# A sparse branch's q, k and v made in the gate part and passed through DRAM, and a merged sum kept in DRAM

## The chip, the cores and the metric

The kernel runs on one core of one Trainium2 chip. The metric is device time in microseconds (us), the median of several runs. The engines are TensorE (PE, with its weight loads PEld), VectorE (DVE), ScalarE (ACT), GpSimd (POOL) and SyncE (SP), which here issues nearly all DMAs, in order. TensorE's granted clock is shown as a share of 2.4 GHz: 1.00 is the upper level, 0.50 the lower one (1.2 GHz).

## The reference

One decoder layer for 1024 tokens of width 1024, with three token mixers over one input projection: A, sparse attention (8 heads of 64; an indexer scores all keys, and each query keeps its 256 best), B, latent attention (8 heads), and M, cross-attention to 256 memory tokens. Each result is multiplied by silu of a gate path and projected to 1024 columns; three sigmoid gates weigh the three, and one output projection goes back to the residual stream.

```python
h = rms_norm(x, g_norm[layer])
proj = h @ w_in[layer]
(q_a, k_a, v_a, q_i, k_i, w_i, z_a, c_q, c_kv, k_rope, z_b, q_m, z_m,
 gate_logits) = jnp.split(proj, split_at, axis=-1)
q_a = partial_rope(rms_norm(q_a.reshape(b, s, A_HEADS, A_HEAD_DIM), g_qn_a[layer]), ...)
k_a = partial_rope(rms_norm(k_a.reshape(b, s, A_HEADS, A_HEAD_DIM), g_kn_a[layer]), ...)
o_a = dsa_attention(q_a, k_a, v_a, q_i, k_i, w_i)      # top 256 keys of each query
...
ys = jnp.stack([o_a * silu(z_a), o_b * silu(z_b), o_m * silu(z_m)], axis=0)
branch = jnp.einsum('nbsw,nwd->nbsd', ys, w_branch[layer])
gates = jax.nn.sigmoid(gate_logits.reshape(b, s, N_BRANCH, D_MODEL))
merged = jnp.einsum('bsnd,nbsd->bsd', gates, branch)
x = x + merged @ w_out[layer]
```

## The kernel before

Every float32 operand is split into a high and a low part (`wsplit`, L246 to L251: ScalarE rounds, VectorE or GpSimd subtracts, as the list `ws` says), and a product is three matmuls (`mm3`, L276 to L279). The transposed normalised input h stays in SBUF all along (tiles hTh, hTl).

The stages follow one another: memory branch; latent branch; the indexer's scores (tiles idx); the gate and branch part; sparse attention; merge and output projection. A framework places the instructions on the engines' queues: program order gives the priority, and an instruction whose operands are expected earlier can be put ahead. Each engine, and SP, then works in the order so fixed.

The **top-k** (`topk_group`) finds the 256th largest score of each row bit by bit: 32 counting passes over six token blocks. Blocks 3, 4 and 6 are counted on ScalarE (tile names ka...), blocks 2, 5 and 7 on VectorE (kd...), L1039. For the upper 16 bits VectorE's passes read bf16 copies (kdh). After the passes each block needs some ten operations of VectorE, and its mask is stored to DRAM (s_msk). `run_topk` hands these steps out: after each group of products it adds the group's planned time on TensorE times TKC (0.44) to an account, and issues steps while the account is positive, each at a planned price. What is left at the end of the part is issued there.

The **gate and branch part**: `branch` for M, then for B. For four blocks of 128 columns it makes z (48 matmuls each), multiplies it with the branch's result (osb, from DRAM) and splits it (tiles yh, yl). Then for eight blocks of output columns and two halves of the tokens it makes a branch product (12 matmuls of 512 columns in a PSUM bank) and multiplies it with the gate (tile tg, from DRAM, two buffers). `emit_b` writes the first branch's result to a sum in SBUF (acc), `emit_m` has GpSimd add the second and stores the sum to DRAM (s_acc). Between them z of branch A is made for three of four blocks (`z_early`, NZG 3) and stored.

The **sparse attention** works by head pairs, 32 units in all (four pairs, two heads, four pairs of token blocks). `qkv_gen` makes q, k and v of a pair (8 token blocks of 24 matmuls with 384 columns), with norms, rotation and split: for the first pair ahead of the loop, for the others in pieces between the units. The filler (`Filler`) puts gate products of branch A between the units, 8 jobs of 16 steps of three matmuls, as many at a place as PFA says. Masks are loaded at the head of the stage (L1385).

In the **merge**, `branch` runs for A: z of the fourth block, the four y tiles, the branch products, the stored sum (tile ac) added, and then the output projection.

## Time and profile before

| | us |
|---|---|
| median of three runs | 1429.53 (1427.94 to 1429.56) |
| span of the profiled execution | 1427.6 |
| TensorE busy | 1366.2 (96%) |
| VectorE busy | 967.5 (68%) |
| ScalarE busy | 687.7 (48%) |
| GpSimd busy | 270.2 (19%) |

The page of the profile gives busy times over the whole span. The questions here are about stages, so the stretches matter: for each, how long TensorE was busy, and at which granted clock. TensorE is never far from busy; what can be won or lost is its idle time and the time at the lower clock.

### The profile page before, as it was taken

The numbers are of one execution on the slowest core, as the hardware profiler recorded it, in microseconds if no ns is written. First come the engines' busy times: TensorE is split into PE (matmuls) and PEld (weight loads), VectorE is DVE, ScalarE is ACT, GpSimd is POOL, SyncE is SP. The second block draws the span as 40 slices with busy tenths as digits, with TensorE's granted clock in tenths as the row PEclk, the third lists the DMA queues.
The fourth block names the chain that finished last, engine by engine and source line by source line (L and its number), as shares of the span: only waits on it lengthen the run. The fifth ranks groups of instructions, "written<-read, shape, count | busy, mean of one in ns | idle before, by whom it ended". The sixth has DMA issues, their size and how long they took to land.

```text
span 1427.6 us, 20798 instructions
## 1 busy us (share of the span) xinstructions
PE 1366.2 (96%) x7440; PEld 1173.0 (82%) x7440; DVE 967.5 (68%) x2409; ACT 687.7 (48%) x1488; POOL 270.2 (19%) x254
## 2 busy tenths in 40 slices
PE   7999999999999999898988998899999999999998
PEld 5998888888888889786867886689899898877887
DVE  5935446678888861479879678777777868836511
ACT  6635433356666651464576563224555535633200
POOL 3150003511102000200232335331202011003200
PEclk9999999999999999999998999999999999999999
DMA  7411222311111120210224325630201001185622
GB/s 245 136 45 52 78 59 86 114 56 41 49 56 53 45 93 20 67 45 23 89 79 151 97 75 182 193 85 9 67 23 45 31 15 45 38 276 184 210 96 74
DMA packets 124631, 122.34 MB, mean 86 GB/s; under 512 B 20336, under 2 KB 90224, under 8 KB 124528
## 3 DMA queue, kind: packets, MB, share of 16 engines
q1 hardware_dynamic: 123952, 118.92, 26.8%
q10 hardware_dynamic: 576, 2.10, 0.4%
q8 instruction: 58, 0.95, 0.3%
q14 instruction: 45, 0.37, 0.1%
HBM read 87.93 MB, written 33.06 MB: 85 GB/s over the span
## 4 chain that ended last, share of the span: by engine, by line
PE 68%; DVE 15%; ACT 6%; issue 4%; DMA 4%; POOL 1%; SPq 1%; ACTq 0%; DVEq 0%; POOLq 0%
PE f L277 5%; PE f L278 5%; PE f L279 4%; DVE kdj L1039 3%; PE a L277 3%; PE a L278 3%; PE a L279 3%; PE o L277 2%; PE o L278 2%; PE o L279 2%; ACT kag L1049 2%; PE br L277 2%; PE br L278 2%; PE br L279 2%; DVE sz L1292 1%
## 5 line engine op out<-in xcount | busy, mean ns | idle before, releaser
L1049 ACT ACTIVATE kag<-idx,kaT 128x512 bf16<-128x512 f32 (+2 forms) x96 | 82.9, 864 | 56.0 <-DVE kaT L1077 39.4
L277 PE MATMUL f<-hTh,f_0h 128*128 128x512 f32 x184 | 77.0, 419 | 1.9 <-ACT f_0h L248 1.2
L277 PE MATMUL f<-hTh,f_1h 128*128 128x512 f32 x184 | 75.6, 411 | 1.3 <-ACT f_1h L248 1.3
L279 PE MATMUL f<-hTh,f_0l 128*128 128x512 f32 x184 | 74.4, 405 | 0.6 <-POOL f_0l L251 0.6
L278 PE MATMUL f<-hTl,f_0h 128*128 128x512 f32 x184 | 74.5, 405 | 0.0
L279 PE MATMUL f<-hTh,f_1l 128*128 128x512 f32 x184 | 74.0, 402 | 0.0
L278 PE MATMUL f<-hTl,f_1h 128*128 128x512 f32 x184 | 73.6, 400 | 0.0
L1568 DVE TENSOR_TENSOR xr<-o,xr 128x512 f32<-128x512 f32 x16 | 11.1, 691 | 64.0 <-PE o L279 64.0
L1223 ACT ACTIVATE irl<-is 128x512 f32<-128x512 f32 (+1 forms) x80 | 37.6, 524 | 24.2 <-DVE idx L1229 15.5
L1526 POOL TENSOR_TENSOR ac<-ac,tg 128x512 f32<-128x512 f32 x16 | 23.5, 1469 | 128.6 <-DMA wo_3r<-in_w_out_dram 109.9
L1039 DVE TENSOR_SCALAR_CACHE_REDUCE kdj<-kdh,kdT 128x384 bf16<-128x384 bf16 (+2 forms) x48 | 46.3, 965 | 0.8
L1039 DVE TENSOR_SCALAR_CACHE_REDUCE kdj<-idx,kdT 128x384 bf16<-128x384 f32 (+2 forms) x48 | 46.2, 963 | 0.6
L369 ACT ACTIVATE fo<-f 128x512 f32<-128x512 f32 x48 | 28.7, 599 | 35.2 <-PE f L279 29.0
L279 PEld LDWEIGHTS f<-hTh,f_0l 128*128 128x128 f32 x184 | 35.2, 191 | 7.9 <-POOL f_0l L251 1.1
L1229 DVE SCALAR_TENSOR_TENSOR idx<-irl,wi,idx 128x1024 f32<-128x1024 f32 (+5 forms) x42 | 40.6, 966 | 1.5 <-ACT irl L1223 0.4
L277 PEld LDWEIGHTS f<-hTh,f_0h 128*128 128x128 f32 x184 | 35.1, 191 | 7.2 <-ACT f_0h L248 1.4
L279 PEld LDWEIGHTS f<-hTh,f_1l 128*128 128x128 f32 x184 | 34.8, 189 | 7.0 <-DVE f_1l L251 0.6
L277 PEld LDWEIGHTS f<-hTh,f_1h 128*128 128x128 f32 x184 | 35.0, 190 | 6.7 <-ACT f_1h L248 2.1
L278 PEld LDWEIGHTS f<-hTl,f_1h 128*128 128x128 f32 x184 | 34.9, 190 | 5.2
L278 PEld LDWEIGHTS f<-hTl,f_0h 128*128 128x128 f32 x184 | 35.3, 192 | 4.3
L1412 ACT ACTIVATE asq<-a 128x256 f32<-128x256 f32 x32 | 12.3, 384 | 51.1 <-PE a L279 50.9
L1266 DVE SCALAR_TENSOR_TENSOR sz<-sz,z 128x512 f32<-128x512 f32 x24 | 16.4, 683 | 27.7 <-ACT sz L1265 27.7
(1215 smaller groups left out, 4862.1 us busy)
## 6 DMA issues: line engine op xcount, KB each, us to landing
s_tg<-fo SPq DMA_DIRECT2D x48, 256.0 KB, 2.0
tg<-s_tg SPq DMA_DIRECT2D x48, 256.0 KB, 3.0
f_0r<-in_w_in_dram SPq DMA_DIRECT2D x23, 256.0 KB, 3.0
f_1r<-in_w_in_dram SPq DMA_DIRECT2D x23, 256.0 KB, 2.9
xx<-in_x_dram SPq DMA_DIRECT2D x8, 512.0 KB, 7.3
osb<-s_o SPq DMA_DIRECT2D x8, 512.0 KB, 3.8
s_acc<-acc SPq DMA_DIRECT2D x16, 256.0 KB, 2.4
ac<-s_acc SPq DMA_DIRECT2D x16, 256.0 KB, 3.4
```

The source lines that it names most:

```text
L277: nc.tensor.matmul(ps, ah, bh, start=start, stop=False)
L278: nc.tensor.matmul(ps, ah, bl, start=False, stop=False)
L279: nc.tensor.matmul(ps, al, bh, start=False, stop=stop)
L369: nc.scalar.activation(o, ps, AF.Tanh, scale=0.5)
L1039: nc.vector.tensor_scalar(out=junk, in0=src[t], scalar1=T[:, i:i + 1], scalar2=0.0, op0=op, op1=ALU.add, accum_out=cnt[:, i:i + 1])
L1049: nc.scalar.activation(junk, idx[t], AF.Sign, bias=T[:, i:i + 1], accum_out=cnt[:, i:i + 1])
L1223: nc.scalar.activation(rl[:, k0:k0 + m], sp[:, 0:m], AF.Relu)
L1229: i_ = nc.vector.scalar_tensor_tensor(out=acc[:, 0:n], in0=rl[:, 0:n], scalar=wc, in1=acc[:, 0:n], op0=ALU.mult, op1=ALU.add)
L1266: zi[0] = nc.vector.scalar_tensor_tensor(out=sz, in0=sz, scalar=1.0, in1=pz[j], op0=ALU.add, op1=ALU.mult)
L1292: i_ = (nc.gpsimd if n and PMUL else nc.vector).tensor_tensor(sz, osb[:, cs], sz, op=ALU.mult)
L1412: nc.scalar.activation(sq.rearrange("p h d -> p (h d)"), ps[:, 0:256], AF.Square)
L1526: nc.gpsimd.tensor_tensor(ac, ac, tg, op=ALU.add)
```

## The change

Four things. The q, k and v of branch A are made by a new function `qkv` inside the gate and branch part, one pair each after the y tiles of the first branch, after those of the second, and twice between the last blocks of z; they are normalised, rotated and split there, stored to DRAM, and loaded in the attention by `load_gen`, the next pair ahead of time (k twice, side by side). The sum of the branches is no longer in SBUF: `emit_b` stores it, `emit_m` loads it, VectorE adds, and it is stored again. The top-k's passes on VectorE all read float32, and a step's planned price and the rate (TKC 0.33) are other. All four blocks of z of branch A are made in the gate part. Beside that: three buffers for tg, osb by halves, own weight buffers for z and branch weights (six), and another spread of the filler (PFA, and FWA weight buffers 6 for 4).

```diff
-TKC = 0.44
+TKC = 0.33
-PFA = (0, 1, 1, 0, 0, 1)
-FWA = 4
+PFA = (1, 1, 1, 0, 0, 1)
+FWA = 6
...
-                yield n / (960 if src is idx else 1900) + 0.1
+                    yield n / 960 + 0.2
...
-            osb = wk.tile([P, S], F32, tag="osb", name=f"osb{n}_{w}", bufs=ob)
-            nc.sync.dma_start(osb, o_T[w * P:(w + 1) * P, :])
+                osb = wk.tile([P, 512], F32, tag="osb", name=f"osb{n}_{w}_{j}", bufs=ob)
+                nc.sync.dma_start(osb, o_T[w * P:(w + 1) * P, cs])
...
         def emit_b(d, j, tg, pb):
-            i_ = nc.vector.scalar_tensor_tensor(out=acc[d][j], in0=tg, scalar=1.0, in1=pb, op0=ALU.add, op1=ALU.mult)
-            run_topk(i_, 2.6 if (2, d) in gates_done else 7.7)
+            i_ = nc.vector.scalar_tensor_tensor(out=tg, in0=tg, scalar=1.0, in1=pb, op0=ALU.add, op1=ALU.mult)
+            nc.sync.dma_start(acc_at(d, j), tg)
+            run_topk(i_, 2.6)
 
         def emit_m(d, j, tg, pb):
-            i_ = nc.vector.scalar_tensor_tensor(out=tg, in0=tg, scalar=1.0, in1=pb, op0=ALU.add, op1=ALU.mult)
-            run_topk(i_, 2.6 if (1, d) in gates_done else 7.7)
-            nc.gpsimd.tensor_tensor(acc[d][j], acc[d][j], tg, op=ALU.add)
-            nc.sync.dma_start(s_acc[d * P:(d + 1) * P, j * 512:(j + 1) * 512], acc[d][j])
+            ac = wk.tile([P, 512], F32, tag="ac", name=f"am{d}_{j}")
+            nc.sync.dma_start(ac, acc_at(d, j))
+            nc.vector.scalar_tensor_tensor(out=tg, in0=tg, scalar=1.0, in1=pb, op0=ALU.add, op1=ALU.mult)
+            i_ = nc.vector.tensor_tensor(tg, tg, ac, op=ALU.add)
+            nc.sync.dma_start(acc_at(d, j), tg)
+            run_topk(i_, 2.6)
+
+        def qkv(p):
+            c = P * p
+            cols = [(C_QA + c, P), (C_KA + c, P), (C_VA + c, P)]
+            ws[:] = WSQ
+            pieces = [wload(wpool, f"a{p}w{kp}", [(wview(w_in, 2 * kp, 2, c0, n), n) for c0, n in cols], 2, 384)
+                      for kp in range(4)]
+            ws[:] = WSG
+            for j in range(2):
+                ...
+                for i in range(4):
+                    tb = 4 * j + i
+                    ps = ps_turn(f"a{p}_{tb}", GAB)[:, 0:384]
+                    for kt in range(NK):
+                        ah, al = h_lhs(kt, tb)
+                        wh, wl = pieces[kt // 2]
+                        mm3(ps, ah, al, wh[:, kt % 2, :], wl[:, kt % 2, :], kt == 0, kt == NK - 1)
+                    ...
+                    nc.scalar.copy(vst[:, i, 0::3, :], pv)
+                    i_ = nc.vector.tensor_tensor(vst[:, i, 1:3, :], pv, f(vst[:, i, 0::3, :]), op=ALU.subtract)
+                    run_topk(i_, 4.2)
+                rsqrt_mean(rr, ss, 1.0 / 64)
+                ...
+                nc.vector.tensor_tensor(qs[:, :, :, 1, :], xq, f(qs[:, :, :, 0, :]), op=ALU.subtract)
+                nc.sync.dma_start(s_va[p][j], f(vst).rearrange("p t e d -> p (t e d)"))
+                nc.sync.dma_start(s_ka[p][j], xk.rearrange("p t h d -> p (t h d)"))
+                nc.sync.dma_start(s_qa[p][j], f(qs).rearrange("p t h e d -> p (t h e d)"))
...
-        branch(2, C_ZM, wpool, wk, yp, s_om, emit_b, run_topk, ob=OBG, mid=lambda: early(0, ZE[0]))
-        branch(1, C_ZB, wpool, wk, yp, s_o[1], emit_m, run_topk, ob=OBG, mid=lambda: early(ZE[0], ZE[1]))
...
+        branch(2, C_ZM, wpool, wk, yp, s_om, emit_b, run_topk, tgb=3, ob=2, mid=lambda: qkv(0))
+        branch(1, C_ZB, wpool, wk, yp, s_o[1], emit_m, run_topk, tgb=3, ob=2, mid=lambda: qkv(1))
+        early(0, 2)
+        qkv(2)
+        early(2, 4)
+        qkv(3)
...
-        def qkv_gen(p):
...
+        def load_gen(p):
             yield 1
+            qs = hd.tile([P, NT, 2, 2, 64], FR, tag="qs", name=f"aqs{p}")
+            kd = hd.tile([P, NT, 2, 2, 64], F32, tag="kd", name=f"akd{p}")
...
+            for j in range(2):
+                for e in range(2):
+                    nc.sync.dma_start(kd.rearrange("p t h e d -> p (t h) e d")[:, 8 * j:8 * j + 8, e],
+                                      s_ka[p][j].rearrange("p (g d) -> p g d", g=8))
+            for src, dst in ((s_qa, f(qs).rearrange("p t h e d -> p (t h e d)")),
+                             (s_va, f(vst).rearrange("p t e d -> p (t e d)"))):
+                for j in range(2):
+                    nc.sync.dma_start(dst[:, 1024 * j:1024 * j + 1024], src[p][j])
```

## Rows read from the trace of the kernel before

**Rows 1.** Stretches: start:end, length, busy us of each engine, PEclk, DMA share, GB/s.
```profile
290.00:505.00 215.00, 214.09 (x1358) 187.16 (x1356) 180.74 (x535) 138.70 (x335) 21.57 (x24) 1.00 0.17 49
...
590.00:672.30 82.30, 74.87 (x347) 58.47 (x347) 71.67 (x118) 45.59 (x93) 8.84 (x11) 0.96 0.16 45
672.30:732.70 60.40, 57.70 (x250) 46.27 (x250) 53.18 (x131) 39.79 (x86) 18.32 (x16) 1.00 0.25 77
732.70:786.60 53.90, 46.56 (x193) 37.98 (x192) 45.57 (x109) 35.00 (x73) 14.14 (x11) 0.91 0.41 134
786.60:842.60 56.00, 56.00 (x241) 45.05 (x241) 39.17 (x86) 32.05 (x67) 20.55 (x16) 1.00 0.27 81
842.60:902.60 60.00, 48.45 (x193) 37.75 (x192) 48.86 (x102) 28.38 (x54) 30.52 (x23) 0.94 0.54 172
902.60:915.40 12.80, 12.77 (x48) 10.29 (x49) 10.54 (x19) 2.21 (x4) 6.48 (x8) 0.87 0.66 203
915.40:953.00 37.60, 35.91 (x194) 35.08 (x193) 27.67 (x70) 10.43 (x23) 7.66 (x8) 0.95 0.31 87
953.00:968.00 15.00, 12.05 (x62) 10.29 (x60) 11.29 (x34) 6.28 (x14) 6.82 (x6) 0.89 0.42 103
968.00:1249.60 281.60, 278.25 (x1714) 252.63 (x1713) 221.99 (x692) 149.90 (x355) 33.66 (x28) 1.00 0.12 35
1249.60:1289.80 40.20, 38.91 (x167) 30.53 (x166) 17.23 (x24) 14.92 (x23) 0.00 (x0) 1.00 0.83 268
1289.80:1334.50 44.70, 44.14 (x193) 35.94 (x192) 28.19 (x40) 15.23 (x24) 20.61 (x15) 1.00 0.58 191
```

**Rows 2.** TensorE's waits, 672.3 to 915.4 us: total, times, longest.
```profile
PE br L277 <- DVE tg L1345: 8.3, 4, 4.3
...
PE br L277 <- DVE acc L1341: 7.3, 1, 7.3
```

**Rows 3.** VectorE's groups, 672.3 to 915.4: count, busy us, mean ns, idle before.
```profile
L1039 DVE TENSOR_SCALAR_CACHE_REDUCE kdj<-idx,kdT 128x1024 bf16<-128x1024 f32 x16 | 20.4, 1274 | 0.2
...
L1039 DVE TENSOR_SCALAR_CACHE_REDUCE kdj<-kdh,kdT 128x1024 bf16<-128x1024 bf16 x11 | 14.0, 1277 | 0.3
```

**Rows 4.** DMA issues over the span: count, KB each, median us to landing.
```profile
tg<-s_tg SPq DMA_DIRECT2D x48, 256.0 KB, 3.0
...
s_acc<-acc SPq DMA_DIRECT2D x16, 256.0 KB, 2.4
...
xqp<-s_qb SPq DMA_DIRECT2D x8, 384.0 KB, 3.3
```

**Rows 5.** VectorE's groups in the sparse attention, 915.4 to 1249.6 us.
```profile
L1413 DVE TENSOR_REDUCE ass<-asq 128x4 f32<-128x256 f32 x32 | 13.3, 417 | 17.9 <-ACT asq L1412 17.7
...
L1444 DVE TENSOR_TENSOR akd<-axk,arr 128x512 f32<-128x512 f32 x16 | 10.8, 683 | 0.2
...
L1419 DVE TENSOR_TENSOR avst<-a,avst 128x128 fp32r<-128x128 f32 x32 | 9.1, 285 | 3.9 <-ACT avst L1418 3.8
...
L426 DVE TENSOR_TENSOR ar_0rp<-axk,cos_a 128x64 f32<-128x64 f32 x8 | 1.8, 224 | 0.0
...
L251 DVE TENSOR_TENSOR a1w0l<-a1w0r,a1w0h 128x768 fp32r<-128x768 f32 x1 | 1.0, 959 | 0.5 <-ACT a1w0h L248 0.5
```

**Rows 6.** Timeline of SP's queue at the end of the top-k.
```profile
937.78 0.32 SPq L1385 DMA_DIRECT2D msk<-s_msk  x1
...
938.15 0.43 SPq L393 DMA_DIRECT2D f_0r<-in_w_in_dram  x1
```

**Rows 7.** Timeline of VectorE, block 6's last part: first and last of nine.
```profile
929.29 1.09 DVE L1085 TENSOR_SCALAR_CACHE_REDUCE kai<-kas 128x896 bf16<-128x896 bf16 x1 [1.08 <-DMA s_msk<-kae]
...
935.60 0.22 DVE L1126 TENSOR_TENSOR kae<-kae,cmask 128x128 bf16<-128x128 bf16 x1
```

**Rows 8.** Timelines on the way into the merge: first load, third y tile's split.
```profile
1249.78 0.32 SPq L1288 DMA_DIRECT2D osb<-s_o  x1
...
1268.31 1.29 DVE L1297 TENSOR_TENSOR yl<-sz,yh 128x512 fp32r<-128x512 f32 x2
```

More of the change, by code (lines that the diff above doesn't have):

```diff
@@ L41 @@
 PFQ = 4
-NZG = 3
 YD = True
@@ L229, in hybrid_kernel @@
     s_acc = dr.tile([D, S], F32, name="s_acc")
+    s_qa, s_ka, s_va = ([[dr.tile([P, n], F32, name=f"s_{c}a{p}_{j}") for j in range(2)] for p in range(4)]
+                        for c, n in (("q", 1024), ("k", 512), ("v", 1024)))
     def rsqrt_mean(dst, ss, inv_n):
@@ L264, in wload @@
             o += w
-        hi = tile(FR, "wp", pool_raw[1], nm + "h")
-        lo = tile(FR, "wp", pool_raw[1], nm + "l")
+        tag, bufs, width = kind or ("wp", pool_raw[1], width)
+        hi = tile(FR, tag, bufs, nm + "h", width)
+        lo = tile(FR, tag, bufs, nm + "l", width)
         wsplit(hi, lo, raw)
@@ L1033, in topk_group, with test @@
         ri = tk.tile([P, nb], I32, name=nm + "r")
[L1035 to L1045 removed]
+        def test():
+            if not act:
+                for i, t in enumerate(ts):
+                    n = (t + 1) * P
+                    junk = tk.tile([P, S], BF, tag="tke", name=f"{nm}j{t}", bufs=1)[:, 0:n]
+                    nc.vector.tensor_scalar(out=junk, in0=idx[t], scalar1=T[:, i:i + 1], scalar2=0.0, op0=ALU.is_ge,
+                                            op1=ALU.add, accum_out=cnt[:, i:i + 1])
+                    yield n / 960 + 0.2
                 return
@@ L1065, in topk_group @@
         nc.vector.memset(T, 0.0)
-        yield from test(high)
+        yield from test()
         if act:
@@ L1072, in topk_group @@
         for b in range(30, -1, -1):
-            yield from test(high if b > 15 else idx)
+            yield from test()
             if act:
@@ L1241, in hybrid_kernel @@
     z_done = set()
+    wkind = [None]
     def z_part(n, w, zc, wpool, wk, zb=2, loaded=None):
@@ L1334, in hybrid_kernel, with acc_at @@
         pool_raw[:] = [2, 8, 768]
-        ap_ = ph.enter_context(tc.tile_pool(name="acc", bufs=1, reuse_waits="tile"))
+        wkind[0] = ("wz", 6, 512)
         yp = ph.enter_context(tc.tile_pool(name="y", bufs=1, reuse_waits="tile"))
         wk = ph.enter_context(tc.tile_pool(name="gwork", bufs=2, reuse_waits="tile"))
-        acc = [[ap_.tile([P, 512], F32, name=f"acc{d}_{j}") for j in range(2)] for d in range(NK)]
+        def acc_at(d, j):
+            return s_acc[d * P:(d + 1) * P, j * 512:(j + 1) * 512]
```

157 lines of the change are left out of this document (49 added, 108 removed).

## The prediction

> **What bounds the kernel now.** I read the busy times first: TensorE has work in 96% of the span, by the table of the page above. The change moves matrix products and adds none, so it can only win time in which TensorE stands still or runs at its lower clock. So I cut the span into stages and looked, in each, at the stage's length, TensorE's busy time and the granted clock [rows 1]. A pace is needed to turn counts into time: the undisturbed z stretch did 240 products of 512 columns in 56.0 us at clock 1.00, that is 0.233 us each; by columns a product of 384 (q, k, v) then needs 0.175 us.
>
> Lost time by stage, [rows 1]: the indexer stretch from 590 us has 82.3 - 74.9 = 7.4 us idle and a clock of 0.96, 3.3 us more: 10.7. The gate and branch part (672.3 to 915.4) needs 528 z and 384 branch products at 0.233 us, 212.8 us, and some 2 us of indexer products; it lasts 243.1, so 28.3 are lost, nearly all in its two branch stretches. The first q, k, v (915.4 to 953) takes 37.6 for 192 x 0.175 = 33.6: 4.0. The start of the attention loop (to 968): 4.6 (3.0 idle, the rest clock). The loop to 1249.6: 3.4 in 282 us. From there to the merge (1289.8): 40.2 for 164 products, 38.3: 1.9. The merge's 192 products take 44.7, nothing lost. Sum: 52.9 us. That is the most that the stretch from 590 us on can give back.
>
> The waits of TensorE say why the branch stretches lose: it waits for VectorE's product of gate and branch (tg, acc) [rows 2]. The granted clock falls to 0.91 and 0.94 in those stretches [rows 1], so each long wait is paid for a second time at the lower clock. Behind the waits are two things. VectorE is busy for 45.6 of 53.9 us there [rows 1], mostly with the top-k's counting passes [rows 3]; and a tg tile has two buffers: the next load (3.0 us, [rows 4]) is issued only after the sum has read the old tile.
>
> **The change, part by part.**
>
> *Counting passes.* The bf16 copies go; all 32 passes of VectorE's group read f32. The row: 128x1024 takes 1277 ns in bf16 and 1274 in f32 [rows 3]. So this costs nothing. The planner however had priced a bf16 pass at half, so in the kernel before it packed twice the work into a planned microsecond; the true prices and the lower rate (0.33 for 0.44) take that pressure away. For a planned 2.6 us of a branch product, the top-k then gets 0.86 us of VectorE at about true price, where before it got 1.14 us of plan, twice that in true time while bf16 lasted. The indexer stretch, where VectorE is busy 71.7 of 82.3 us [rows 1], gets about half the passes: I take 8 us lost for 10.7 (6 to 11).
>
> By the Trainium skill (VectorE: DVE Perf Modes, section The perf-mode tier table) a tensor_scalar in bf16 runs at four elements a cycle and in f32 at two. It would make 16 f32 passes of the three tiles cost some 23 us of VectorE more than the bf16 ones, an estimate from that ratio and the rows; the counting form in this trace shows no difference at all, so the sum leaves it out.
>
> *q, k, v into the gate part.* 768 products, 134.4 us of TensorE, leave the attention stage, and the last 48 products of z (11.2 us) leave the way into the merge. Both go into the gate part: 212.8 + 145.6 = 358 us of products there. Their cost is zero only if VectorE follows. Per token block of 4.2 us TensorE it has four operations, 0.42 and three of 0.28 to 0.29, 1.27 us [rows 5], 1.1 for its share of rotation, scaling and splitting (a quarter of twelve operations of about 0.25 and two of 0.68), 0.5 for its share of the weight splits (four of 0.96 for eight blocks [rows 5]) and 1.4 planned us of top-k: 4.3, just full. The branch stretches have room (0.68 + 0.86, in the second 1.36 + 0.86, of 2.8 us), the z stretches more. The sum over the part: the 197 us busy of now, plus about 100 of moved work at the same overlap, is under 300 of 358.
>
> *The sum in DRAM, three tg buffers.* Now 16 stores and 16 loads more, and the add moves from POOL to VectorE (0.68 us a piece). A tg tile lives for its load, 3.0 us, the products, 1.4, and a store of 2.4 [rows 4], with waits about 7.5: over three buffers 2.5 us, just under the 2.8 us of one branch product. Each store waits on SP for VectorE's add, and behind it in SP's order stand the next loads of tg, sum and branch weights, for which TensorE waits. The bytes stay under the work: 10 MB written for q, k, v and 8 MB moved for the sum, in a part whose branch stretches already ran at 134 and 172 GB/s [rows 1]; q, k, v add 24 stores and 32 loads on SP, at some 0.4 us of issue [rows 6] 22 us of a queue that is idle most of 600 us. I take 12 us lost in the gate part for 28.3. Bounds: 5, as in its z stretches (3 to 4 lost in 129 us), and 25, if the round trip of the sum paces the second branch.
>
> *The boundary to the attention.* Before, the first q, k, v hid the end of the top-k: its last tile ran until 935.8, the mask was stored, the load of it issued at 937.8, and the filler's weights behind that on SP [rows 6], all under products. Now nothing of that kind follows the last q, k, v. The plan's accounts: 340 planned us (before: 195; q, k, v 134 and the fourth z 10 more) x 0.33 = 112 units; the steps' planned prices are 92 for VectorE's passes and 35 for the rest, less 10 done in the indexer, 117. So 5 are left over. The last tile needed nine operations, 6.1 us of VectorE between 929.3 and 935.8 [rows 7], for 3.5 units: 1.7 us a unit. The last q, k, v carries 11 units, 19 us, beside its own 23 us, in 33.6 us: VectorE comes out 8 us late, 8.5 more for the rest, then the mask's store and load, 2.4 + 3.0 by tiles of that size [rows 4]: 22 us after the last product. K too must come from DRAM (bounded by the nearest load, 3.3 us for 384 KB in pieces of 384 bytes [rows 4]) and can't before the weights' memory is free. Against that stand one filler job (48 products, 11 us) and 3 us of transposes and scores. That leaves 8 us, and the clock falls: with the first chain of softmax I take 14 us lost, for 8.6 now (4.0 + 4.6). Bounds 3 and 28: no backlog, or filler weights that queue behind the masks on SP, as in [rows 6].
>
> By the Trainium skill (DMA: Bandwidth & Descriptors, Specifications) pieces under 512 bytes fall below line rate; K is read in pieces of 256. If that doubled the load it would cost some 3 us, once, an estimate; the row with pieces of 384 bytes shows 3.3 us, no such doubling, and the other pairs are loaded far ahead.
>
> *The attention loop* loses the q, k, v work of TensorE, VectorE and ACT alike. What is left per unit is the filler, spread wider (115 of 128 steps inside it, 82 before), and its own products. The nearest stage is the latent branch's loop, built the same way, 0.9 us idle in 215 at 181 us of VectorE [rows 1]; the sparse loop has 222.0 us of VectorE now [rows 1], loses some 70 (24 token blocks at 1.27 + 1.1, the two heads' K scaling, the filler's splits, which fall to POOL) and keeps about 150 in about 200 us (281.6, less 100 of q, k, v, plus 18 of filler). I take 4 us for 3.4 (0 to 12).
>
> *Into the merge.* Here cover is given away: 116 filler products and the 48 of z, 38 us [rows 1], stand there now while the last heads are stored, loaded, multiplied and split; 13 filler steps, 9 us, remain. The loads begin where the attention ends, at 1249.8, and the first three of four y tiles are ready 20 us on [rows 8]; now in halves with two buffers, about 21 us to the last. 9 us of filler and up to 10 us of partial sums in five banks cover most: I take 7 lost for 1.9 (1 to 16).
>
> Sum: 8 + 12 + 14 + 4 + 7 = 45 for 52.9, 8 us less. The profiled span is 1427.6 and the median of the runs 1429.5, 1.9 above. 1427.6 - 8 + 1.9 = 1421.5 us.
>
> **The rivals.**
> Cover everywhere: top-k in time at the boundary (6), gate part 7, merge 3, indexer 8, loop 3: 27 lost, 26 gained, 1403.5. For it: VectorE has 60 us of room over the gate part. Against it: the end of the top-k is where the room isn't.
> Slower, the boundary: the top-k's backlog holds the masks, SP holds the filler's weights behind them, and TensorE stands for the whole 22 us and pays the clock: 30 lost there, 1437.5. It decides against the change from about 25 us on. For it: the order on SP in [rows 6]. Against it: the filler could be loaded first.
> The round trip: the second branch stays paced by its loads, as now: gate part 25 lost, 1434.5. For it: 2.5 us against 2.8 is thin and SP issues in order.
> The change doesn't do what it says, because the order of issue leaves the stretches as they are: 1429.5.
> The Trainium skill's f32 rule (VectorE: DVE Perf Modes), with 23 us more of VectorE on the path, would give up to 1444; with 1277 against 1274 ns it gets no chance.
>
> **How the numbers follow.** Forecast 0.45 (1413 to 1430 by its own bounds), cover 0.20, boundary 0.20, round trip 0.12, nothing 0.03. The range 1403 to 1440 reaches from the cover rival to a little beyond the boundary one. A measurement tells about 0.2%, 2.9 us, from no change. Faster: three quarters of the forecast, all of the cover case and a little of the others, 0.59; within: 0.15; slower: 0.26.
>
> **What would show it.** Right: TensorE's waits for tg and acc down from 15.6 us to a few, clock near 1.00 in the branch stretches; a TensorE gap of about 10 us with a fall of the clock after the last q, k, v, ended by masks or K; some 7 us idle ahead of the merge's first branch product. Wrong: branch stretches that still wait for tg or for the sum's loads; a boundary over 25 us (then it is slower); or no gap at either place (then 1403). If the loop itself idles by more than 12 us, my comparison with the latent branch's loop is at fault.

## The result and the profile after

The changed kernel takes 1475.98 us (1474.21 to 1480.0, four runs) where the kernel before takes 1428.74 beside it: 1.034 times as long, with a 95% interval of 1.0321 to 1.036. The forecast was 1421.5, the range ended at 1440. The profiled execution has a span of 1473.8 us, 46.2 more than before.

First the page of the profile after: busy times over the span, and the DMA line.

```profile
PE 1374.4 (93%) x7440; PEld 1173.9 (80%) x7440; DVE 952.7 (65%) x2381; ACT 682.2 (46%) x1465; POOL 261.3 (18%) x248
...
DMA packets 153960, 154.86 MB, mean 105 GB/s; under 512 B 38400, under 2 KB 108288, under 8 KB 153856
```

TensorE has the same 7440 matmuls as before, and the other engines less work; TensorE is busy 8 us longer and its share fell from 96 to 93%, so the loss is idle time and low clock again. The DMAs move 154.86 MB where they moved 122.34. The stretches of the changed kernel, with the columns of [rows 1]: the indexer; the whole gate and branch part; in it the first branch, the z of the second, the second branch, the first z of branch A and the fourth q, k, v; the boundary, up to the first transposed probabilities; the attention loop; the way into the merge; the merge's products.

```profile
590.00:672.00 82.00, 74.22 (x356) 59.61 (x356) 69.33 (x107) 47.62 (x100) 4.47 (x9) 0.97 0.16 48
...
672.00:1058.80 386.80, 367.06 (x1727) 317.76 (x1726) 263.40 (x699) 171.43 (x363) 106.08 (x88) 0.98 0.44 138
...
752.00:800.00 48.00, 44.92 (x194) 35.86 (x193) 29.66 (x89) 22.56 (x50) 12.19 (x10) 1.00 0.61 194
800.00:851.60 51.60, 45.95 (x193) 35.67 (x193) 35.38 (x67) 24.51 (x48) 17.20 (x13) 1.00 0.51 146
...
887.00:937.70 50.70, 46.77 (x193) 36.45 (x191) 35.84 (x96) 19.67 (x42) 15.94 (x15) 0.97 0.69 225
937.70:967.00 29.30, 25.25 (x97) 20.43 (x98) 18.79 (x43) 14.97 (x28) 3.65 (x4) 0.88 0.64 194
...
1024.80:1058.80 34.00, 33.99 (x193) 33.63 (x191) 24.51 (x76) 9.15 (x20) 4.36 (x4) 1.00 0.21 76
1058.80:1102.80 44.00, 14.83 (x48) 11.04 (x49) 28.52 (x67) 9.26 (x18) 7.81 (x8) 0.57 0.68 193
1102.80:1302.40 199.60, 198.22 (x1227) 167.79 (x1226) 157.91 (x459) 123.35 (x273) 18.02 (x14) 1.00 0.29 84
1302.40:1325.20 22.80, 9.27 (x41) 7.21 (x39) 11.87 (x18) 7.83 (x13) 0.00 (x0) 0.81 0.86 280
1325.20:1381.00 55.80, 50.42 (x193) 37.86 (x194) 31.13 (x41) 16.14 (x25) 24.41 (x15) 0.93 0.66 212
```

Read by the prediction's own rule (idle time, and busy time at the lower clock; for the gate part and the merge length less products at 0.233 us, 0.175 for q, k, v):

| stretch | lost before | forecast | lost after |
|---|---|---|---|
| indexer | 10.7 | 8 | 7.8 idle, 2.2 by the clock: 10.0 |
| gate and branch part | 28.3 | 12 | 386.8 - 358.4 = 28.4 |
| boundary to the attention | 8.6 | 14 | 29.2 idle, 6 by the clock: 35 |
| attention loop | 3.4 | 4 | 1.4 |
| into the merge, and its products | 1.9 | 7 | 78.6 - 231 x 0.233 = 24.8 |
| sum | 52.9 | 45 | 99.6 |

The sum grew by 46.7, the span by 46.2. Two places hold it, the boundary (+26) and the merge (+23), and the gate part gave nothing back. TensorE's waits (total, times, longest) name what stands there; the first row is the boundary's, the second the merge's, the others the gate part's.

```profile
PE akt L1442 <- DMA akd<-s_ka: 21.5, 2, 16.3
...
PE br L273 <- ACT b0w0h L241: 13.6, 1, 13.6
...
PE z L273 <- ACT kag L1042: 4.2, 1, 4.2
PE z L275 <- POOL z1w_4l L244: 4.1, 3, 2.0
PE br L273 <- DVE tg L1327: 3.8, 5, 2.6
...
PE br L273 <- DVE tg L1320: 0.9, 1, 0.9
```

The 8.3 and 7.3 us of [rows 2] are down to 3.8 and 0.9. At the boundary the queue of SP shows why TensorE stood 16.3 us for K of the first pair, which had lain in DRAM for 300 us (timeline: start, length, DMA):

```profile
1059.02 1.31 SPq L1426 DMA_DIRECT2D akd<-s_ka  x2
1066.35 0.33 SPq L1113 DMA_DIRECT2D s_msk<-kde  x1
...
1071.46 0.32 SPq L1378 DMA_DIRECT2D s_ka<-a_1xk  x1
...
1073.49 0.32 SPq L1379 DMA_DIRECT2D s_qa<-a_1qs  x1
1073.85 0.53 SPq L1426 DMA_DIRECT2D akd<-s_ka  x1
1077.41 0.33 SPq L1113 DMA_DIRECT2D s_msk<-kae  x1
1077.78 0.53 SPq L1426 DMA_DIRECT2D akd<-s_ka  x1
...
1086.09 0.32 SPq L1113 DMA_DIRECT2D s_msk<-kae  x1
...
1088.14 0.32 SPq L1412 DMA_DIRECT2D msk<-s_msk  x1
1088.50 0.81 SPq L389 DMA_DIRECT2D f_0r<-in_w_in_dram  x1
```

The second half of K is loaded at 1073.85 and 1077.78, behind two mask stores and the stores of the last pair's k and q; the filler's weights, which should have covered the boundary, come last of all, at 1088.5. And each mask store waits for VectorE, here the last operations of blocks 7 and 6; the third line is the first use of a mask:

```profile
1066.10 0.21 DVE L1112 TENSOR_TENSOR kde<-kde,cmask 128x128 bf16<-128x128 bf16 x1
...
1085.83 0.23 DVE L1112 TENSOR_TENSOR kae<-kae,cmask 128x128 bf16<-128x128 bf16 x1
...
1093.15 0.69 DVE L490 CUSTOM_DVE_ANT_0 a_3p<-a_3S,msk 128x512 f32<-128x512 f32 x1 [2.79 <-DMA msk<-s_msk]
```

So two chains end here side by side: the top-k's backlog (VectorE until 1086.1, 27 us after the last product), and the loads behind the stores. Of TensorE's 29.2 idle us, 21.5 are put down to K, 4.7 to the masked scores and 2.8 to q. In the merge the same queue shows the branch weights, for which TensorE waits, behind the last of eight half tiles of the attention's result, and behind the first of four loads of the output projection's weights:

```profile
1316.74 0.42 SPq L258 DMA_DIRECT2D wo_0r<-in_w_out_dram  x1
1319.54 0.32 SPq L1278 DMA_DIRECT2D osb<-s_o  x1
1319.91 0.43 SPq L258 DMA_DIRECT2D b0w0r<-in_w_branch_dram  x1
```

### The profile page after: what moved, and what is told of

Read it like the earlier page. It is cut to its first block, busy times and chain, and to the rows that moved or that the text cites. A ratio compares the mean times of both kernels' runs of the same rounds, so it can differ in the third digit from the quotient of the medians.

```text
span 1473.8 us, 20906 instructions
## 1 busy us (share of the span) xinstructions
PE 1374.4 (93%) x7440; PEld 1173.9 (80%) x7440; DVE 952.7 (65%) x2381; ACT 682.2 (46%) x1465; POOL 261.3 (18%) x248
## 2 busy tenths in 40 slices
DMA packets 153960, 154.86 MB, mean 105 GB/s; under 512 B 38400, under 2 KB 108288, under 8 KB 153856
## 4 chain that ended last, share of the span: by engine, by line
PE 61%; DVE 16%; DMA 7%; ACT 7%; issue 4%; POOL 3%; SPq 0%; ACTq 0%; DVEq 0%; POOLq 0%
PE f L273 6%; PE f L275 5%; PE f L274 5%; DVE kdj L1036 3%; ACT kag L1042 3%; PE o L273 2%; PE o L274 2%; PE o L275 2%; DVE sz L1280 1%; PE br L275 1%; PE br L273 1%; PE ixps L274 1%; PE ixps L275 1%; PE ixps L273 1%; PE br L274 1%
## 5 line engine op out<-in xcount | busy, mean ns | idle before, releaser
L1036 DVE TENSOR_SCALAR_CACHE_REDUCE kdj<-idx,kdT 128x384 bf16<-128x384 f32 (+2 forms) x96 | 92.5, 963 | 0.9
L1559 DVE TENSOR_TENSOR xr<-o,xr 128x512 f32<-128x512 f32 x16 | 11.1, 691 | 65.9 <-PE o L275 61.0
L244 POOL TENSOR_TENSOR f_0l<-f_0r,f_0h 128x512 fp32r<-128x512 f32 (+1 forms) x10 | 14.0, 1396 | 212.3 <-ACT f_0h L241 179.9
L1209 ACT ACTIVATE irl<-is 128x512 f32<-128x512 f32 (+1 forms) x80 | 37.6, 525 | 16.4 <-DVE idx L1215 12.8
L244 POOL TENSOR_TENSOR f_1l<-f_1r,f_1h 128x512 fp32r<-128x512 f32 (+1 forms) x10 | 14.0, 1398 | 153.8 <-ACT f_1h L241 112.7
L1215 DVE SCALAR_TENSOR_TENSOR idx<-irl,wi,idx 128x1024 f32<-128x1024 f32 (+5 forms) x42 | 39.9, 949 | 2.0 <-ACT irl L1209 0.2
L1254 DVE SCALAR_TENSOR_TENSOR sz<-sz,z 128x512 f32<-128x512 f32 x24 | 16.4, 684 | 38.0 <-ACT sz L1253 38.0
```

The costliest lines, as they stand in the source:

```text
L244: eng.tensor_tensor(lo, raw, f(hi), op=ALU.subtract)
L1036: nc.vector.tensor_scalar(out=junk, in0=idx[t], scalar1=T[:, i:i + 1], scalar2=0.0, op0=ALU.is_ge, op1=ALU.add, accum_out=cnt[:, i:i + 1])
L1209: nc.scalar.activation(rl[:, k0:k0 + m], sp[:, 0:m], AF.Relu)
L1215: i_ = nc.vector.scalar_tensor_tensor(out=acc[:, 0:n], in0=rl[:, 0:n], scalar=wc, in1=acc[:, 0:n], op0=ALU.mult, op1=ALU.add)
L1254: zi[0] = nc.vector.scalar_tensor_tensor(out=sz, in0=sz, scalar=1.0, in1=pz[j], op0=ALU.add, op1=ALU.mult)
```

## Experiments

The kernel before stood at 1428.9 to 1430.5 us beside these, and one kernel's runs lie 1 to 7 us apart, so small differences of medians between two lines say little; the stretches come from one execution each. The table gives stretches of each profile in us: from the first z product to the last product ahead of the attention (gate), from there to the first transposed probabilities (boundary), from there to the end of the loop, and from there to the last branch product (merge).

| kernel | gate | boundary | loop | merge | median |
|---|---|---|---|---|---|
| changed | 387.7 | 44.0 | 199.6 | 78.6 | 1476.0 |
| e_tkc40 | 410.0 | 27.6 | 203.4 | 80.4 | 1484.9 |
| e_swap | 396.9 | 39.9 | 199.7 | 80.8 | 1483.3 |
| e_tkc40_swap | 408.3 | 21.3 | 203.4 | 79.8 | 1482.2 |
| e_bits | 397.1 | 27.6 | 203.4 | 77.8 | 1473.2 |
| e_tkc0 (one run) | 428.9 | 27.4 | 203.7 | 78.5 | 1506.3 |
| e_3bits | 378.8 | 26.7 | 203.4 | 79.3 | 1453.9 |
| e_noam | 384.3 | 43.8 | 199.6 | 78.6 | 1471.8 |
| e_z3 | 378.2 | 46.1 | 199.9 | 77.9 | 1467.0 |
| c_merge | 376.6 | 43.1 | 199.6 | 90.1 | 1475.0 |
| c_z3ob | 377.6 | 45.4 | 199.9 | 74.6 | 1464.4 |
| c_wfirst | 377.9 | 45.5 | 199.6 | 80.5 | 1471.8 |

In the last four kernels the gate part has 11.2 us of products less.

**The boundary: backlog or order on SP.**

```diff
-TKC = 0.33
+TKC = 0.40
```

> The changed kernel with the rate of the top-k at 0.40 instead of 0.33 and nothing else. Theory A, the top-k's backlog holds the boundary: 340 planned us x 0.40 = 136 units for the 117 that the steps need, so the plan ends some 48 planned us before the last product of q, k, v and the masks are in DRAM by then. The 44 us between the last product of q, k, v and the first transposed probabilities then fall to some 20 (K's load, transposes, scores, one softmax); the gate part pays up to 5 us for the denser passes. 1476.0 - 24 + 5 = about 1457. Theory B, the order on SP holds it: K's and q's loads stand behind the last pair's stores of k and q, which end some 15 us after the last product whatever the top-k does; TensorE still waits 16 us for K, and at most 8 us are won: 1468 or more. Neither: 1476.

Measured 1484.9, slower than the changed kernel. The boundary did fall, by 16.4 us of theory A's 24, but the gate part took 22.3 us more, not 5:

```profile
672.00:1080.90 408.90, 374.41 (x1727) 322.69 (x1726) 281.04 (x727) 172.80 (x364) 106.93 (x88) 0.97 0.43 134
1080.90:1108.50 27.60, 9.75 (x41) 7.40 (x42) 11.58 (x38) 6.40 (x12) 5.93 (x7) 0.69 0.75 208
```

VectorE has 17.6 us more work in the gate part (281.0 for 263.4), and the part is 22 us longer, though VectorE still idles 31% of it. Its room there was on paper only. What is left of the boundary is mostly theory B's: TensorE still waits 13.2 us for K. And of the 16.4 us won, 3.8 come back behind it: in the five kernels with less backlog the loop takes 203.4 to 203.7 us, in part because products that ran in the boundary now fall into it (1235 for 1227 here).

```diff
         qkv(2)
-        early(2, 4)
         qkv(3)
+        early(2, 4)
```

> The changed kernel with the last q, k, v made ahead of the last two blocks of z instead of behind them, nothing else. The top-k's units are the same, so its backlog at the end of the part is the same 5 units, but the last pair's own norms, splits and stores are done 22 us earlier. Theory B (SP's order: K's loads stand behind the last pair's stores): the 16.3 us wait for K falls to about 5, the masks are then what is late; 10 us won, 1466. Theory A (the top-k's backlog): the last mask still lands some 25 to 30 us after the last product, because VectorE has the same passes to do there; 3 to 5 us won, since VectorE has less beside them: 1471 to 1473.

> Both edits: the rate of the top-k at 0.40 and the last q, k, v ahead of the last two blocks of z. With neither masks nor the last pair's stores at the end, only K's load, its transposes and the first softmax are left after the last product: theory A and B both give a boundary of 15 to 18 us for 44, and 1476 - 27 + 4 = about 1453. If A alone is right it is no better than the rate alone; if B alone is right, no better than the order alone; if they stand one behind the other, it is the only one of the three that wins more than 15 us.

In the changed kernel the fourth q, k, v stands behind the last block of z, not ahead of it. The order alone takes 4.1 us off the boundary, the rate alone 16.4, both 22.7: two chains, of which the backlog is the longer, and neither alone is the whole. With the order alone, K comes sooner (9.4 us of waits for 21.5) and TensorE waits for a mask instead:

```profile
PE a_3S L1472 <- DVE a_3mx L490: 13.3, 1, 13.3
```

Both runs missed in the total, 1483.3 and 1482.2, because the gate part again took back 9 and 21 us. With the order alone that is mostly where two q, k, v now follow each other, 75 us for the 67 of their products.

```diff
-        for b in range(30, -1, -1):
+        for b in range(30, -1 if act else 15, -1):
```

> The changed kernel with VectorE's group of the top-k stopping after the upper 16 bits: the lower 16 of its 32 counting passes are left out (the threshold of token blocks 2, 5 and 7 is then only settled to its upper half). That takes some 16 x 3.3 = 53 us off VectorE, all of the backlog at the end of the gate part included, with the density of the passes before that unchanged. Theory A (VectorE's backlog holds the boundary): the 44 us between the last q, k, v product and the first transposed probabilities fall to about 20, and the late stretches of the gate part lose a few us less: about 1448. Theory B (K's and q's loads stand on SP behind the last pair's stores, which wait for POOL and VectorE for 15 us): 8 us less at most, 1468.

Measured 1473.2. The boundary is 27.6 us, as with the higher rate, where theory A said 20: 13.5 us of waiting for K are left. The total missed, for the gate part grew by 9 us although VectorE has 28 us less to do in it. With VectorE's group done early, the plan's units go to ScalarE's group: the second branch has 36.9 us of ScalarE where it had 19.7, and takes 60.1 us for 50.7. Less work in the same queues did not mean less waiting.

**What holds the gate part.**

```diff
-TKC = 0.33
+TKC = 0.0
```

> The changed kernel with the rate of the top-k at 0: no step of it is handed out in the gate part, all are issued behind it. The total says nothing (150 to 200 us of VectorE then stand bare at the boundary: 1600 to 1680); the number is the length of the gate part, from the first z product to the last of the fourth q, k, v: 387.7 us in the changed kernel for 358 us of products. If VectorE's and ScalarE's passes, put between the part's own steps, are what TensorE waits behind, it falls to about 365 to 370. If SP's order and the round trip of the sum set it, it stays above 380.

The premise failed: with no step handed out, the framework itself put the passes into the gate part, the last on VectorE at 871 us. VectorE has 254.7 us of work between 672 and 1044, and the part takes 428.9 us. It tells one thing, from one run: the passes without pacing cost it 41 us more, for a boundary like that of the rate of 0.40.

```diff
-        for b in range(30, -1, -1):
+        for b in range(30, 27, -1):
```

> The changed kernel with both groups of the top-k stopping after 4 of their 32 counting passes (the thresholds are coarse, so other keys are kept); rate, steps after the passes and all else unchanged. It takes some 90 us of VectorE's and most of ScalarE's passes away. Theory D (the passes between the part's own steps, on two queues that work in order, are what TensorE waits behind): the gate part, 387.7 us for 358 us of products, falls to about 365, the boundary from 44 to about 27 as where the backlog was gone: 1476 - 22 - 17 = 1437. Rival E (the part's own work on VectorE, ScalarE, GpSimd and SP, now with q, k, v in it, holds TensorE without any top-k): the gate part stays above 378: 1450 or more.

Measured 1453.9, on the rival's side. The top-k now ends at 769 us (its last mask is stored), within the first part below; the second part has none of it:

```profile
671.10:808.40 137.30, 129.90 (x577) 110.08 (x578) 81.74 (x186) 45.25 (x88) 43.30 (x34) 0.95 0.46 143
808.40:1049.90 241.50, 236.92 (x1153) 210.27 (x1151) 93.26 (x233) 53.64 (x109) 61.84 (x54) 0.99 0.47 146
```

The second part holds the same products as 800.0 to 1058.8 in the changed kernel, 235.2 us by the pace: it loses 6.3 us where that lost 23.6. The first, with the passes that are left and all the masks' operations in it, loses 8 more than in the changed kernel; why is not shown. So theory D holds where the passes are gone, and 17 of the gate part's 28 us are lost with them there; the whole part, 378.8, is 9 us shorter and came out on the rival's side of the bound. Most of the 6.3 us that stay are the second branch's, which still has its round trip (46.1 us for 44.8), and a wait of 2.8 us for the z behind it.

```diff
-            ac = wk.tile([P, 512], F32, tag="ac", name=f"am{d}_{j}")
-            nc.sync.dma_start(ac, acc_at(d, j))
-            nc.vector.scalar_tensor_tensor(out=tg, in0=tg, scalar=1.0, in1=pb, op0=ALU.add, op1=ALU.mult)
-            i_ = nc.vector.tensor_tensor(tg, tg, ac, op=ALU.add)
+            i_ = nc.vector.scalar_tensor_tensor(out=tg, in0=tg, scalar=1.0, in1=pb, op0=ALU.add, op1=ALU.mult)
```

> The changed kernel without the reading half of the sum's round trip: the second branch stores its own product and the 16 loads of the first branch's sum and the 16 additions are left out, so the first branch is missing from the merged sum. My forecast took the round trip as nearly free (12 us lost in the gate part in all), the rival gave it 25. If the round trip paces the second branch, its 192 products take 45 us for 50.7, the z behind it starts at once, and 8 to 10 us are won: 1467. If VectorE's queue is what it waits for, VectorE is 11 us lighter there and 3 us are won: 1473.

Measured 1471.8, 4.2 us won: the second branch fell from 50.7 to 46.0 us. The round trip costs that, between the two expectations. Load and addition went together here, so the run does not part them; and e_3bits reached 46.1 with the round trip kept, so it costs this only beside the passes.

**The merge: cover, order or bytes.**

```diff
-        early(2, 4)
+        early(2, 3)
```

> The changed kernel with z of the fourth block made in the merge again, as in the kernel before, and nothing else. Theory C, the lost cover costs the merge: 11.2 us of z products stand where TensorE now idles 13.6 us for the first branch weights, so the way into the merge (1302.4 to 1381.0, 78.6 us for 54 us of products) takes about 80 us with 65 us of products, some 10 us lost instead of 24.6. The gate part is 11.2 us shorter, but the top-k loses 10.2 x 0.33 = 3.4 units, some 6 us more at the boundary. Sum: 1476.0 - 11 + 2 + 6 = about 1472, and the merge's own loss is the number to look at. Rival: the loads queue on SP for other reasons, the fourth y tile now also waits for its own z, and the merge loses the same 24 us: 1482.

Measured 1467.0, 9 us won. 279 products (65.1 us) in 77.9: 12.8 us lost for 24.8. What is left is 11.1 us of waiting for that block's own weights.

```diff
-        early(2, 4)
+        early(2, 3)
-PFA = (1, 1, 1, 0, 0, 1)
-FWA = 6
-OB5 = 2
+PFA = (0, 1, 1, 0, 0, 1)
+FWA = 4
+OB5 = 4
```

> The changed kernel with the merge's cover put back: z of the fourth block made in the merge, the filler spread as in the kernel before (its first place 0, weight buffers 4), and four buffers for the half tiles of the attention's result. Theory C (the lost cover costs the merge): some 38 us of products then stand where the y tiles are loaded and made, as before, and the way into the merge loses 3 us for 24.6; the shorter gate part costs the boundary 6: 1476 - 22 + 4 = about 1458. Rival: the filler steps taken out of the loop leave holes there (the loop's VectorE and ScalarE are what it runs at), 10 us or more come back as idle time in the loop: 1467, as with z alone.

Measured 1475.0, which neither expected: theory C was nearer on the merge, the rival right on the loop. The merge's 356 products (83.1 us) took 90.1, 7 lost. But the loop, rid of 72 filler products (16.8 us by the pace), is not a microsecond shorter (first row here; the changed kernel's is above):

```profile
1091.60:1291.20 199.60, 190.00 (x1155) 158.80 (x1155) 159.61 (x459) 120.49 (x269) 14.65 (x11) 0.98 0.26 75
```

The loop has a length of its own, 199.6 us, and the filler that the change puts there rides free. It fills it, too: TensorE is then busy for 198.2 of the 199.6 us.

```diff
-        early(2, 4)
+        early(2, 3)
-OB5 = 2
+OB5 = 4
```

> The changed kernel with z of the fourth block in the merge (which alone gave 1467.0) and four buffers instead of two for the half tiles of the attention's result in the merge; the filler's spread is left as changed. If two buffers make the chain of loads, products and splits there, the 12.8 us that the way into the merge still loses fall to 5 to 8 and the time to 1460 to 1463. If the loads themselves or the order of the weights behind them set it: 1466 to 1468.

Then, on top of that edit:

```diff
+        zfirst = z_part(n, 3, zc, wpool, wk, zb) if n == 0 else None
         for w in range(4):
-            szs = z_part(n, w, zc, wpool, wk, zb)
+            szs = zfirst if n == 0 and w == 3 else z_part(n, w, zc, wpool, wk, zb)
```

> The changed kernel with z of the fourth block in the merge, four buffers for the half tiles (which together gave 1464.4), and that block's z issued ahead of the other three y tiles, so that its weights are among the first loads behind the attention. If the order on SP is what TensorE waits for, the 8.1 us between the last filler product and the first z product fall to 4 or less and the time to 1457 to 1460. If the weights' memory or the loads of the last head's result come late in any case, nothing moves: 1463 to 1466.

The buffers won 2.6 us (1464.4, between the two expectations; 9.5 us lost in the merge). The order missed: the wait for z's weights did fall, from 8.1 to 1.7 us, but the time rose to 1471.8. The stretches from the end of the loop, c_z3ob and then c_wfirst, show where it went:

```profile
1292.40:1323.40 31.00, 22.84 (x90) 17.71 (x89) 14.20 (x20) 10.34 (x16) 0.00 (x0) 0.83 0.85 272
1323.40:1367.00 43.60, 43.60 (x193) 36.09 (x193) 27.51 (x41) 14.71 (x23) 18.97 (x14) 1.00 0.68 205
```

```profile
1294.70:1317.40 22.70, 20.91 (x90) 16.25 (x89) 11.71 (x17) 8.58 (x14) 0.00 (x0) 1.00 0.89 283
1317.40:1375.20 57.80, 49.66 (x193) 37.57 (x193) 35.00 (x45) 17.77 (x28) 24.03 (x15) 0.94 0.65 205
```

The branch products now wait for the high and low parts of their own weights. The last columns tell of bytes: 283 GB/s with the DMA engines 89% busy. From the end of the loop to the last branch product the changed kernel moves 78.6 us x 232 GB/s = 18.2 MB, the kernel before 19.3 MB [rows 1]. The highest rate found over 40 us in these traces is 301 GB/s, in e_3bits:

```profile
901.50:941.50 40.00, 35.43 (x147) 28.20 (x146) 18.49 (x26) 3.73 (x6) 8.63 (x10) 0.96 0.95 301
```

At that rate 18.2 MB need 60 us. Before, they ran under 83 us of products; in the changed kernel only 54 are left. That the loads are short of cover is shown; that no order of them could do is not. Four loads of w_out, 0.5 MB each, serve the output projection, and the first stands ahead of the first branch weights (1316.74 above). Without them 16 MB need 53 us. An order with them last was not tried, so how much of the merge's loss is order and how much bytes stays open.

**Pieces of the change made alone in the kernel before.**

```diff
-        branch(2, C_ZM, wpool, wk, yp, s_om, emit_b, run_topk, ob=OBG, mid=lambda: early(0, ZE[0]))
-        branch(1, C_ZB, wpool, wk, yp, s_o[1], emit_m, run_topk, ob=OBG, mid=lambda: early(ZE[0], ZE[1]))
+        branch(2, C_ZM, wpool, wk, yp, s_om, emit_b, run_topk, tgb=3, ob=OBG, mid=lambda: early(0, ZE[0]))
+        branch(1, C_ZB, wpool, wk, yp, s_o[1], emit_m, run_topk, tgb=3, ob=OBG, mid=lambda: early(ZE[0], ZE[1]))
```

> The kernel before with three buffers for tg in both branches of the gate part and nothing else: one piece of the change alone. My step said that the two buffers make the branch stretches wait (15.6 us of waits for tg and acc, and the clock that falls behind them). If so, 8 to 12 us are won: 1417 to 1421. Rival: VectorE, busy 85% of those stretches with the counting passes, is what paces them, and a third buffer only moves the wait: 1427 to 1431.

With that and `emit_b` and `emit_m` as in the change:

> The kernel before with the sum of the branches in DRAM as in the change: three tg buffers, 16 stores and 16 loads more, the addition on VectorE instead of GpSimd; q, k and v and everything else as before. My step took the round trip as hidden: then this is as good as three buffers alone, within 3 us. Rival (the round trip paces the second branch): its 16 branch products take 60 us or more as before, and the time is 8 to 15 us above that of the three buffers alone. VectorE's 16 additions of 0.68 us cost at most 11 us if nothing hides them.

Three buffers alone: 1427.3, ratio 0.9982 (0.997 to 0.9994); the rival was right, the first branch takes 54.3 us as before, and the second, up to the z product behind it, 60.2 us for the 60.0 of [rows 1]. With the sum in DRAM as well: 1432.6, ratio 1.0017 (1.0007 to 1.0027), 5.3 us worse, most of it in the second branch: more than the 3 us of a hidden round trip, less than the rival's 8. First b_tg3's second branch, up to its last branch product, then b_sum's:

```profile
842.90:898.00 55.10, 48.08 (x193) 37.80 (x191) 43.53 (x90) 26.02 (x51) 29.00 (x21) 0.94 0.53 166
```

```profile
844.00:905.30 61.30, 50.47 (x193) 39.00 (x192) 49.57 (x110) 26.80 (x53) 14.62 (x11) 0.89 0.65 206
```

```diff
-                nc.vector.tensor_scalar(out=junk, in0=src[t], scalar1=T[:, i:i + 1], scalar2=0.0, op0=op,
+                nc.vector.tensor_scalar(out=junk, in0=idx[t], scalar1=T[:, i:i + 1], scalar2=0.0, op0=op,
```

> The kernel before with the upper 16 of VectorE's counting passes reading the float32 scores instead of their bf16 copies, planned prices and all else unchanged. By the rows (1274 against 1277 ns for 128x1024) this changes nothing: 1427 to 1431. If a bf16 pass were in truth cheaper, or a float32 pass slowed others by what it reads, the gate part's VectorE would carry up to 23 us more and the time would be 8 us or more longer.

Measured 1425.9, ratio 0.9972 (0.9962 to 0.9982): no cost, a small gain instead. It sits in the gate part (4 us) and is not explained.

```diff
-TKC = 0.44
+TKC = 0.55
...
-                yield n / (960 if src is idx else 1900) + 0.1
+                yield n / 960 + 0.2
...
-        yield from test(high)
+        yield from test(idx)
...
-            yield from test(high if b > 15 else idx)
+            yield from test(idx)
...
```

> The kernel before with one part of the change made alone and its rate set to suit: VectorE's passes all read float32 at their true price (n/960 + 0.2), with a rate of 0.55 so that the plan still ends about where it did (195 x 0.55 = 107 of 117 units), and three buffers for tg. Theory: the half price of the bf16 passes put some 2.3 us of true work on VectorE for a branch product of 2.8 us, beside 0.7 of its own; at the true price it is 1.7 + 0.7, and the first branch falls from 54 us to 47, the second by 3 to 5: 1417. Rival: the tail of the top-k (10 units) comes out behind the first q, k, v and the boundary takes back what is won: 1425 to 1430.

And against c_topk:

```diff
-TKC = 0.55
+TKC = 0.57
...
-            run_topk(i_, 2.6 if (2, d) in gates_done else 7.7)
+            run_topk(i_, 2.0)
-            run_topk(i_, 2.6 if (1, d) in gates_done else 7.7)
+            run_topk(i_, 2.0)
-            bg(zi[0], 5.1)
+            bg(zi[0], 6.0)
-                    bg(zi[0] if n and PMUL else i_, 5.1)
+                    bg(zi[0] if n and PMUL else i_, 6.0)
```

> The kernel before with float32 passes at their true price and three tg buffers, as in the last run of that kind, and the passes shifted: 2.0 planned us for a branch product (2.6), 6.0 for half a z block (5.1), rate 0.57, in all 196 x 0.57 = 112 of 117 units. If the passes on VectorE pace the branch products and z has room for them, the two branch stretches fall from 51.5 and 52.5 us to about 48 each, the z stretches stay at 44 and 45, the backlog at the boundary halves: 1417. If the room in the z stretches is not there (VectorE waits in them for ScalarE), z grows by what the branches lose: 1423 to 1427.

The first gave 1424.6, ratio 0.9958 (0.9943 to 0.9972), just below the rival's range: the branches fell to 51.5 and 52.5 us, the gate part ended 11 us earlier, and the rival took 8 of them back: the boundary went from 19.6 to 27.3. Shifting the passes to the z stretches (c_topk2) gave 1432.9, ratio 1.003: z did not grow, the second branch did, to 60.8 us, with waits of up to 2 us for weights and y where it starts and then one of 8.3 for tg. Neither expectation: fewer passes planned for a product did not make it faster. What sets its pace, beyond VectorE coming late to it, stays open.

```diff
...
-            for t in ts:
-                high[t] = tk.tile([P, (t + 1) * P], BF, name=f"{nm}h{t}")
-                nc.vector.tensor_copy(high[t], idx[t].bitcast(BF).rearrange("p (n u) -> p n u", u=2)[:, :, 1])
+            pass
...
```

> The kernel before with the two pieces that each won a little alone, prices and rates as they were: VectorE's passes all read float32 (the bf16 copies are not made) and tg has three buffers. If their gains add (1425.9 and 1427.3 alone against 1429.9), 1422 to 1424. If both free the same wait (VectorE late for the first product of a branch stretch), no more than the better one: 1425 to 1427.

Together with the float32 source and three tg buffers this gave 1422.3 us, ratio 0.9958 (0.9943 to 0.9972). That is what the two gains together would give (0.9954), but the interval reaches to the float32 source alone (0.9972), so that they add is not shown. By the ratio it is level with c_topk; these two are the fastest kernels here, and neither holds one of the change's two large moves, q, k, v in the gate part and the sum in DRAM.

## Why the prediction was wrong

**The boundary** is the term that decided. It was given 14 us with bounds of 3 and 28, and lost 35. Its parts: the backlog was estimated at 8 + 8.5 us of VectorE after the last product and then the mask's store and load, 22 in all; VectorE in fact worked for 27, and the mask was used 34 us after the last product. The step that failed most is the cover: "one filler job (48 products, 11 us) and 3 us of transposes and scores" stood against the 22. Almost none of it came in time. The filler's weights were issued at 1088.5, behind every mask, and K, which I had bounded by 3.3 us of load, stood behind the last pair's stores: 21.5 of the 29 idle us are waits for it. The rival on the boundary had the filler's half of this mechanism (SP holds its weights behind the masks, and the clock falls), from [rows 6], and put it at 30, without K; I gave it 0.20 because "the filler could be loaded first", which the code's order did not say. The list of what would show me wrong had it too: over 25 us, then slower.

**Into the merge** was given 7, bounds 1 and 16, and lost 24.8. I counted latencies (20 us to the y tiles) against cover in filler and partial sums. The partial sums could not start, since their weights came behind the y loads (and the first of w_out); and bytes were not counted at all: the 40.2 us at 268 GB/s stood in [rows 1], and 18 MB at such a rate need 68 us, more than the 54 us of products left. e_z3 and c_merge, the latter with four buffers, show the cover's worth, 12 and 18 us of the 25.

**The gate part** was given 12, bounds 5 and 25, and lost 28.4. What was said of the waits for tg came true (15.6 us down to 4.7, clock at 0.97 to 1.00 in the branches), but not for the reason given: three buffers alone change nothing there (b_tg3), and with the denser passes of e_tkc40 11 us of those waits come back. The failed step is the room on VectorE, "under 300 of 358" us busy, by which it would follow at no cost: VectorE did 263 us of 387 and did not follow. That the passes cost the part its time is shown: 17.6 us of them more cost 22 us of time (e_tkc40), and where they were gone 17 came back (e_3bits). Why, at 68% busy, is argued: it and ScalarE work in order and wait for each other (VectorE waits 38 us in the part for ScalarE's step of z). The round trip of the sum, taken as hidden, costs 4 to 5 us with its addition on VectorE (e_noam, b_sum); the rival that paced the whole branch with it was too large.

**The attention loop** (4 forecast, 1.4 found) was right, and by more than I knew: its length did not hang on the filler. **The counting passes** were right: float32 costs no more than bf16 (b_f32src). By the Trainium skill (VectorE: DVE Perf Modes, The perf-mode tier table) bf16 would have been twice as fast; the run shows no such cost. **The indexer** (8 forecast, 10.0 found) did not gain from the lower rate.

**K's load** was bounded by a row with pieces of 384 bytes, and I wrote of "no such doubling". The DMA issues of the changed kernel (count, KB each, median us to landing):

```profile
akd<-s_ka SPq DMA_DIRECT2D x16, 256.0 KB, 5.4
aqs<-s_qa SPq DMA_DIRECT2D x8, 512.0 KB, 4.7
avst<-s_va SPq DMA_DIRECT2D x8, 512.0 KB, 5.6
```

K in pieces of 256 bytes takes longer than q with twice the bytes, but v, with twice the bytes too and in pieces as long as q's, takes longer still. The Trainium skill (DMA: Bandwidth & Descriptors, Specifications) says that pieces under 512 bytes fall below line rate; these rows neither show it nor speak against it, since they do not part the pieces from other traffic, and a load of K in longer pieces was not tried; at the boundary the place in the queue cost more than the load.

**The range** took one large miss at a time. The upper bounds of the five terms, 11, 25, 28, 12 and 16, add up to 92 us lost, which is 1469 us, while the stated range stopped at 1440; the gate part, the boundary and the merge each passed its own bound, so the measured 1476 lies above both.

What stays open: why e_bits, with less for VectorE to do, lengthens the gate part by 9 us (the denser ScalarE passes are argued, not shown), where the 4 us of b_f32src come from, and what another order of the merge's loads would win.

## What to carry to other kernels

Work that leaves a stage takes its cover with it: before moving products, list what hides under them (the end of a background task, loads by bytes at the highest rate a row shows, weights), and look at the in-order DMA queue for what each next load stands behind. The idle share of an engine that works in order need not be room; ask what one more microsecond on it costs where it would go, and try that alone first. A stage that keeps its length when its filler is taken out is the right place for filler, until TensorE is full there.

## What the runs showed of the hardware

The waits at the boundary and ahead of the merge were paid twice, as TensorE came back at the lower clock: 0.57 granted over the 44 us of the boundary, of which it stood idle for 29. A counting pass over 128x1024 cost the same from float32 as from bf16, and a kernel with float32 alone was 0.28% faster. The DMA engines reached 280 to 283 GB/s at 86 to 89% busy for 23 us in the loads behind the attention, and 301 at 95% for 40 us around the end of e_3bits's second branch.

VectorE's smallest operations stretch while GpSimd works on a tile. Timelines of c_topk2, VectorE's first and then GpSimd's: an operation on 128x3 takes 0.16 us alone and 1.20 beside a GpSimd addition. Of the 166 elementwise operations on 128x3 in this trace, the 108 that met no GpSimd instruction all took under 0.2 us, and 33 of the 58 that did took over 0.5.

```profile
863.73 0.16 DVE L1072 SCALAR_TENSOR_TENSOR kaT<-kar,kaT 128x3 int32<-128x3 int32 x1
...
874.28 1.20 DVE L1072 SCALAR_TENSOR_TENSOR kdT<-kdr,kdT 128x3 int32<-128x3 int32 x1
```

```profile
874.17 1.29 POOL L1342 TENSOR_TENSOR acc<-acc,tg 128x512 f32<-128x512 f32 x1
```

The Trainium skill (Trainium Architecture — The Big Picture, What this means for kernel authors) says that VectorE and GpSimd share a port pair under an exclusive lock; the rows agree. It is one more way in which work on two queues can lengthen the passes; what it costs in all was not measured.
